# Bringing seven parts of x through ScalarE's DMA queue in a hybrid encoder layer

## The chip, the cores and the metric

The kernel runs on one core of a Trainium2 chip. The core has a matrix engine, TensorE (PE in the profile, with PEld for its weight loads), a vector engine, VectorE (DVE), ScalarE (ACT), GpSimd (POOL) and SyncE (SP). Each engine works through its own instruction queue in order. Data moves between the large memory (DRAM) and the on-chip memory by DMA; an engine's queue issues a DMA with an instruction of its own, and 16 DMA engines carry it out. Here SyncE issues nearly all DMAs and ScalarE issues some stores.

The metric is the time of one execution on the device in microseconds, as the median of several runs. Lower is better.

## The reference, cut to what matters

The kernel computes one layer of a bidirectional encoder for a sequence of 2048 positions and 1024 channels, in float32, and a final norm:

```python
h = rmsnorm(x, norm_w)                                   # x: 2048 x 1024
proj = h @ w_in                                          # w_in: 1024 x 10240, ten splits of 1024
q, f_fwd, f_bwd, i, g_a, u, v, g_b, m_a, m_b = split(proj)
# branch A: gated linear recurrence, 8 heads of 128, chunks of 64, forward and backward
k, log_f = forget(f, lower_bound)                        # per direction
state_t  = diag(f_t) state_{t-1} + k_t v_t^T ;  o_t = state_t^T q_t      # v is i
y_a = rmsnorm(o_fwd + o_bwd, gnorm_w) * silu(g_a)
# branch B: spatial gating over chunks of 128 positions
y_b = gelu(u) * (w_s @ layernorm(gelu(v)) + b_s) * silu(g_b)
merged = sigmoid(m_a) * (y_a @ w_proj_a) + sigmoid(m_b) * (y_b @ w_proj_b)
out = rmsnorm(x + merged @ w_out, final_norm_w)
```

Most of the work is in the products with `w_in`. The change lies in how the operand of these products that comes from h is brought on chip.

## The kernel before, in words

**Products.** Each large product is done in float16 with a high and a low half of each operand (three matmuls for one: high by high, high by low, low by high). It is also cut in 2 x 2 blocks by a scheme with seven block products in place of eight (`PRODUCTS`). Each of the seven needs one *part* on the x side: the blocks A11, A12, A22, and the sums S1 to S4 of blocks. A part holds 128 partitions x 8 KB, 1 MB in all. The sequence is cut into two halves, p = 0 and p = 1, and each has its own seven parts. They are made once at the start and kept in DRAM (`x_d`; the page calls the tensors `x` and `x_sums`, and the on-chip tile `xT`).

**Slots.** There are eight slots on chip for parts: seven in use and one spare. A *group* (`seven`, L1108) is seven products, in the order 0, 1, 2, 3, 5, 4, 6, for one unit of 256 weight columns and one half p. One product is `mm12` (L1171 holds the matmul): 12 matmuls of 128 x 512. Product 6 of a group is held back and done after the first two products of the next group (the "tail").

**Phases.** The value stage (`values`) and the recurrence (`recurrence`) go through groups of the same p in *phases*: the recurrence has nine phases, of two, then seven times three, then four groups, and p changes from each to the next. In the last group of a phase, as soon as a product has read a part for the last time, its slot is free, and the next part of the *other* p is loaded into it. `after` (L584) does this: it is called after each product of each group; if the group is the last of its phase (`end`), it takes the slot of the part just read and calls `x_fetch` (L578) for the part after it in `PARTS`. The seventh slot becomes the spare one. A11 of the other p goes into the spare slot, asked for at the beginning of the group before the last (L555). `after` also asks for pieces of the next group's weights (L586), on SyncE's queue.

**The recurrence beside it.** Between products, `pump` runs steps of the recurrence itself for one head, direction and segment of 512 positions at a time: operands (scans on VectorE, activations on ScalarE), scores on PE (`sc`), masking, state updates on PE (`pu`, L918) and outputs on PE (`po`). For the state updates the keys are needed transposed: `key_parts` copies kt to float16 on ScalarE (L839), takes the rest on VectorE (L840), and issues a DMA transpose into `ks` on SyncE's queue (L842). SyncE's queue in this stage also carries the stores and loads of intermediate outputs and scores (`of`, `o_d`, `at`) and of values (`v`).

**Copies out of PSUM.** A product's result leaves the accumulation memory (PSUM, tiles `bank`) by ScalarE: as a plain copy for products 0, 1 and 2 (L1119, which notes itself as `self.reads["act"]`), or with a scale at L605 in product 6; products 3, 5 and 4 leave by VectorE (L1207).

**What sets the order.** The framework's planner arranges each engine's instructions by their place in the program (which `high_priority` can raise) and by its own estimate of when each becomes ready, and puts in the semaphore waits. The order on each engine is then fixed. A DMA that overwrites a slot waits, in the queue of the engine that issues it, until the matmuls that read the slot are done. `tc.issue_after(ins)` puts the block's instructions on the engine of `ins` behind it.

Of the kernel before, what the change touches and what calls it, by code (L numbers as in the profile page):

```python
# [53 lines left out]
A11, S1, A12, A22, S3, S2, S4 = B11, T1, B21, B22, T2, T3, T4 = range(7)  # L54
# [5 lines left out]
class Trunk:  # L60
# [89 lines left out]
    def plan(self):  # L150

        w = self.w_in
        self.todo, self.us_i = [(w, C_I + U * hp) for hp in range(4)], {}
        self.made, self.hooks, self.reads, self.fill = [], [], {}, []
        self.reads_first, self.ahead_of, self.wt, self.junk, self.few = True, 0, None, None, {}
# [357 lines left out]
    def recurrence(self):  # L513
        nc, tc = self.nc, self.tc
        with ExitStack() as es:
            E = es.enter_context
            R = dict(side="right", reuse_waits="tile")
            self.c1 = E(tc.tile_pool(name="g_const", bufs=1, **R))
            self.gv = E(tc.tile_pool(name="g_v", bufs=2, **R))
            self.gq = E(tc.tile_pool(name="g_q", bufs=1, **R))  # L520
            self.gof = E(tc.tile_pool(name="g_of", bufs=7, **R))
            self.gat = E(tc.tile_pool(name="g_at", bufs=5, **R))
            self.gt = E(tc.tile_pool(name="g_t", bufs=2, **R))
            self.gs = E(tc.tile_pool(name="g_s", bufs=11, **R))
            self.zs = E(tc.tile_pool(name="zsr", bufs=9, reuse_waits="tile"))
            self.pk = E(tc.tile_pool(name="p_k", bufs=1, space=PSUM, reuse_waits="tile"))
            self.pq = E(tc.tile_pool(name="p_r", bufs=1, space=PSUM, reuse_waits="tile"))
            self.reads_first, self.ahead_of = False, READS
            self.q_free, self.q = [f"q{n}" for n in range(12)], {}
            self.fill, self.late_norm = [], None  # L530
            self.queue, self.state, self.kept_at, self.v_of, self.v_raw = [], {}, {}, {}, {}
            self.pipe, self.turn, self.credit, self.held_once = [None] * 2, 0, 0.0, False
            self.patterns()

            groups = []
            for hp in range(4):
                a, b = hp % 2, 1 - hp % 2
                if hp == 0:
                    groups.append([("q", 0, 0, 0, None), ("f", 0, 0, 1, None)])
                groups.append([("q", hp, 1, a, ("b", hp)), ("f", hp, 1, b, ("q", hp + 1) if hp < 3 else ("mb", 0)),  # L540
                               ("b", hp, 1, a, None)])
                if hp < 3:
                    groups.append([("q", hp + 1, 0, b, None), ("b", hp, 0, a, ("f", hp + 1)),
                                   ("f", hp + 1, 0, a, None)])
            groups.append([("b", 3, 0, 1, ("mb", 1)), ("mb", 0, 0, 0, ("mb", 2)), ("mb", 1, 0, 1, ("u", 0)),
                           ("mb", 2, 0, 0, ("gb", 0))])
            tail = None
            for n, phase in enumerate(groups):
                p, last = n % 2, n == len(groups) - 1
                for m, (kind, hp, _, slot, after) in enumerate(phase):  # L550
                    end = m == len(phase) - 1 and not last
                    g = self.r_group(kind, hp, p, slot)
                    done = partial(self.after, slot, after, p, end)
                    if m == len(phase) - 2 and not last:
                        self.x_fetch(1 - p, A11, self.spare)  # L555
                    first = list(self.ORDER[:2])
                    for i in self.ORDER[:2]:
                        next(g)
                        done(i)
                        self.pump()  # L560
                    if tail:
                        next(tail[0])
                        tail[1](6)
                        self.pump()
                    for i in self.ORDER[2:6]:
                        next(g)
                        done(i)
                        self.pump()
                    tail = g, done
            next(tail[0])  # L570
            tail[1](6)
            while self.queue or any(self.pipe):
                self.step_on(True)
            self.norms()
            self.X = [{c: self.slot_part(self.slot[p, c]) for c in self.PARTS} if p == 0 else {} for p in range(2)]
        self.reads_first, self.ahead_of, self.pq = True, 0, None

    def x_fetch(self, p, part, slot):  # L578
        self.nc.sync.dma_start(out=slot, in_=self.x_d[p][part])
        self.slot[p, part] = slot  # L580

    def after(self, slot, key, p, end, n):

        if key and n in self.LOADS:  # L584
            at = slice(*self.LOADS[n])
            self.nc.sync.dma_start(out=self.ws[slot][:, :, at], in_=self.pre[key].d[:, :, at])  # L586
        if end:
            i = self.ORDER.index(n)
            free = self.slot.pop((p, self.PARTS[i]))
            if i < 6:  # L590
                self.x_fetch(1 - p, self.PARTS[i + 1], free)
            else:
                self.spare = free

# [1713 lines left out]
```

## Time and profile before

| | |
|---|---|
| median of 3 runs | 2207.83 us (2206.01 to 2208.66) |
| profiled execution, its own time | 2207.17 us |
| its span, first to last instruction | 2205.4 us |
| mean granted clock of TensorE | 0.996 |
| TensorE / VectorE / ScalarE / GpSimd busy | 98% / 76% / 61% / 15% of the span |
| stores of the value stage's results (L1324) | issued from 216.5 to 350.1 us |
| transposes of the recurrence (L842) | 64, issued from 385.8 to 1024.9 us |

"Busy" is the time in which an engine's instructions run, as a share of the span. Each row of a group of instructions gives its line in the kernel, engine, operation, what it writes and reads, the count, busy time, the mean length of one in ns, and the idle time just before them with what ended it. A row of waits gives who waited, for whom, the total, how often, and the longest. In rows of the timeline the start and the length stand ahead. Engine names with a q (SPq, ACTq) are instructions of that engine's queue which occupy its sequencer alone, such as the issue of a DMA; "to landing" is the time from a DMA's issue until its data has arrived.

### The profile page before, as it was taken

The page shows a single profiled execution, that of the slowest core. Times are in us where ns is not written, and L with a number is a line of the kernel's source. Part 1 is how long each engine was busy: PE and PEld are TensorE (multiplying, and loading weights), DVE is VectorE, ACT ScalarE, POOL GpSimd, SP SyncE. Part 2 cuts the span into 40 slices and gives each one's busy share as a digit, 9 for nine tenths or more (in the row PEclk, how much of TensorE's full clock was granted, in tenths as well). Part 3 has the DMA queues.
Part 4 walks back from the last instruction along what each step waited for, and adds up shares of the span by engine and source line. Part 5 has one row for each costly group of instructions (what it writes and reads, how often), then busy time and mean ns, then how long its engine had stood idle before and what let it go on. Part 6 is the DMA issues. An engine that isn't in the chain of part 4 may idle for free.

```text
span 2205.4 us, 35017 instructions
## 1 busy us (share of the span) xinstructions
PE 2161.6 (98%) x12654; PEld 1216.1 (55%) x12654; DVE 1665.7 (76%) x3063; ACT 1347.2 (61%) x2740; POOL 338.0 (15%) x526
## 2 busy tenths in 40 slices
PE   8999999999999999999999999999999999999998
PEld 7887444666666666666454554444445444444444
DVE  6878965878999889988677684698864745687764
ACT  6577876767778778777465554676664622344442
POOL 2036643002303103213000000000000000000011
PEclk9999999999999999999999999999999999999999
DMA  8898996768768758867732224788756665877643
GB/s 324 335 354 313 360 376 249 192 177 256 217 161 255 221 154 237 251 168 216 251 112 94 82 86 148 286 291 315 285 178 206 239 234 185 280 262 281 247 157 105
DMA packets 269064, 503.91 MB, mean 228 GB/s; under 512 B 92496, under 2 KB 154192, under 8 KB 245200
## 3 DMA queue, kind: packets, MB, share of 16 engines
q1 hardware_dynamic: 245696, 459.36, 62.7%
q10 hardware_dynamic: 23184, 42.22, 5.1%
q8 instruction: 101, 1.65, 0.3%
q14 instruction: 83, 0.68, 0.1%
HBM read 317.74 MB, written 166.99 MB: 220 GB/s over the span
## 4 chain that ended last, share of the span: by engine, by line
PE 44%; issue 3%; DMA 2%; DVE 1%; ACT 0%; POOL 0%; SPq 0%; POOLq 0%; DVEq 0%; ACTq 0%
PE bank L1171 43%; PE px L1501 1%; DMA mg<-zs 1%; DVE seven L1071 1%; DMA raw<-mg 0%; PE px L1805 0%; DMA seven<-kept 0%; DVE zs L1207 0%; DMA zs<-mb 0%; ACT seven L1070 0%; DVE tmp L973 0%; ACT tmp L1021 0%; POOL wsb L1026 0%; DVE zs L1973 0%; DVE zs L1961 0%
## 5 line engine op out<-in xcount | busy, mean ns | idle before, releaser
L1171 PEld LDWEIGHTS <-seven 128*128 128x128 f16 x7404 | 722.8, 100 | 767.0 <-issue 10.3
L1171 PE MATMUL bank<-xT,seven 128*128 128x512 f16 x4116 | 972.1, 380 | 4.8 <-ACT zs L605 2.5
L1171 PE MATMUL bank<-seven 128*128 128x512 f16 (+1 forms) x2028 | 436.1, 378 | 1.0 <-DVE zs L2027 0.7
L1171 PE MATMUL bank<-xs,seven 128*128 128x512 f16 x1260 | 282.2, 379 | 0.0
L1207 DVE SCALAR_TENSOR_TENSOR zs<-bank,us,zs 128x512 f32<-128x512 f32 x192 | 142.7, 745 | 91.2 <-PE bank L1171 64.8
L1119 ACT ACTIVATE zs<-bank,us 128x512 f32<-128x512 f32 x192 | 130.2, 680 | 106.6 <-PE bank L1171 101.3
L1174 PEld LDWEIGHTS sc<-ff,kt 128*128 128x128 f32 x684 | 130.0, 190 | 47.8
L1215 ACT ACTIVATE zs<-zs 128x512 f32<-128x512 f32 x144 | 90.0, 627 | 102.8 <-DVE zs L1207 90.8
L1071 DVE SCALAR_TENSOR_TENSOR seven<-raw,ws,seven 128x1024 f16<-128x1024 f32 x80 | 111.1, 1419 | 50.8 <-ACT seven L1070 49.9
L1171 PE MATMUL bank<-seven,xT 128*128 128x512 f16 x672 | 146.5, 379 | 1.2 <-DVE zs L1207 1.2
L220 PE MATMUL pin<-wsplit,xT 128*128 128x256 f16 x512 | 140.2, 274 | 2.2 <-DVE xT L302 2.2
L219 PE MATMUL pin<-wsplit,xT 128*128 128x256 f16 x512 | 140.2, 274 | 0.9 <-DVE wsplit L208 0.9
L218 PE MATMUL pin<-wsplit,xT 128*128 128x256 f16 x512 | 140.4, 274 | 0.0
L1119 ACT ACTIVATE zs<-bank,su 128x512 f32<-128x512 f32 x72 | 49.0, 682 | 142.8 <-PE bank L1171 132.3
L850 ACT ACTIVATE q<-ff,e 128x64 f32<-128x64 f32 x512 | 131.6, 337 | 1.6 <-issue 0.4
L1174 PE MATMUL sc<-ff,kt 128*128 128x64 f32 (+1 forms) x684 | 119.2, 256 | 0.0
L1171 PEld LDWEIGHTS <-xT 128*128 128x128 f16 x672 | 64.6, 98 | 77.2 <-issue 1.5
L1207 DVE SCALAR_TENSOR_TENSOR zs<-bank,su,zs 128x512 f32<-128x512 f32 x72 | 53.8, 748 | 52.1 <-PE bank L1171 41.7
L1070 ACT ACTIVATE seven<-raw,ws 128x1024 f16<-128x1024 f32 x80 | 88.3, 1138 | 6.3 <-DVE ws L147 2.8
L1071 DVE SCALAR_TENSOR_TENSOR seven<-tmp,ws,seven 128x768 f16<-128x768 f32 x80 | 82.1, 1056 | 10.8 <-ACT seven L1070 10.4
L926 DVE SCALAR_TENSOR_TENSOR st<-st,e,pu 128x128 f32<-128x128 f32 x224 | 75.9, 339 | 6.0 <-PE pu L918 4.9
L1040 POOL TENSOR_TENSOR tmp<-raw 128x512 f32<-128x512 f32 x40 | 59.6, 1490 | 108.3 <-DVE seven L1071 40.1
(272 smaller groups left out, 3192.9 us busy)
## 6 DMA issues: line engine op xcount, KB each, us to landing
xT<-x_sums SPq DMA_DIRECT2D x41, 1024.0 KB, 7.1
raw<-in_w_in_dram SPq DMA_DIRECT2D x38, 1024.0 KB, 8.2
xT<-x SPq DMA_DIRECT2D x30, 1024.0 KB, 7.2
seven<-kept SPq DMA_DIRECT2D x15, 1792.0 KB, 9.1
kept<-seven SPq DMA_DIRECT2D x16, 1024.0 KB, 5.1
kept<-seven SPq DMA_DIRECT2D x16, 768.0 KB, 6.1
v<-v SPq DMA_DIRECT2D x20, 512.0 KB, 5.6
x<-xT SPq DMA_DIRECT2D x8, 1024.0 KB, 8.4
```

The lines of the kernel that those rows point to most:

```text
L218: nc.tensor.matmul(ps, lh(k), rh(k), start=start and k == 0, stop=False, skip_group_check=len(ks) < KT)
L219: nc.tensor.matmul(ps, lh(k), rl(k), start=False, stop=False, skip_group_check=len(ks) < KT)
L220: nc.tensor.matmul(ps, ll(k), rh(k), start=False, stop=k == KT - 1, skip_group_check=len(ks) < KT)
L850: self.nc.scalar.activation(out=q0[:, at], in_=ff[:, at], func=AF.Copy, scale=e8[:, n, b:b + 1])
L926: nc.vector.scalar_tensor_tensor(out=sn, in0=st, scalar=e8[:, n, last:last + 1], in1=pu[:, n, :], op0=ALU.mult, op1=ALU.add)
L1070: nc.scalar.activation(out=out[0], in_=src, func=AF.Copy, scale=s)
L1071: nc.vector.scalar_tensor_tensor(out=out[1], in0=src, scalar=s, in1=out[0], op0=ALU.mult, op1=ALU.subtract)
L1119: self.reads["act"] = self.nc.scalar.activation(out=t, in_=ps, func=AF.Copy, scale=su)
L1171: nc.tensor.matmul(ps, lhs(x, k), rhs(y, k), start=start and not (k or n), stop=k == 3 and n == 2, skip_group_check=True)
L1174: self.fill.pop(0)()
L1207: self.reads["dve"] = self.nc.vector.scalar_tensor_tensor(out=more, in0=ps, scalar=su, in1=more, op0=ALU.mult, op1=ALU.add)
L1215: self.nc.scalar.activation(out=out, in_=more, func=func)
```

## The change

`x_fetch` gets an argument by which it issues the load from ScalarE's queue. `after` and the phase loop no longer call it at once; they note the wanted load in `next_x`. A new function `x_next`, called at the beginning of each `after`, issues the noted load from ScalarE's queue, behind the newest plain copy out of PSUM. The loads of whole parts in the value stage's last group for p = 1 and in all phase changes of the recurrence go this way. The other callers of `x_fetch` (the loads at the start, A11 ahead of the recurrence, and those after the recurrence) stay on SyncE's queue.

```diff
     def plan(self):
+        self.next_x = None
...
                     if m == len(phase) - 2 and not last:
-                        self.x_fetch(1 - p, A11, self.spare)
+                        self.next_x = 1 - p, A11, self.spare
...
-    def x_fetch(self, p, part, slot):
-        self.nc.sync.dma_start(out=slot, in_=self.x_d[p][part])
+    def x_fetch(self, p, part, slot, beside=False):
+        (self.nc.scalar if beside else self.nc.sync).dma_start(out=slot, in_=self.x_d[p][part])
         self.slot[p, part] = slot
 
+    def x_next(self):
+
+        if self.next_x:
+            with self.tc.issue_after(self.reads["act"].ins):
+                self.x_fetch(*self.next_x, True)
+            self.next_x = None
+
     def after(self, slot, key, p, end, n):
 
+        self.x_next()
         if key and n in self.LOADS:
...
             free = self.slot.pop((p, self.PARTS[i]))
             if i < 6:
-                self.x_fetch(1 - p, self.PARTS[i + 1], free)
+                self.next_x = 1 - p, self.PARTS[i + 1], free
             else:
                 self.spare = free
```

## The prediction

> **What bounds the kernel now.** I read the page first: how busy each engine is, and what each hardware DMA queue carried (q1 is SyncE's, q10 ScalarE's).
>
> ```profile
> PE 2161.6 (98%) x12654; PEld 1216.1 (55%) x12654; DVE 1665.7 (76%) x3063; ACT 1347.2 (61%) x2740; POOL 338.0 (15%) x526
> q1 hardware_dynamic: 245696, 459.36, 62.7%
> q10 hardware_dynamic: 23184, 42.22, 5.1%
> ```
>
> TensorE (PE) is busy 98% of 2205.4 us. A change that adds and removes no matmul can only change PE's idle time and its clock, and may also add idle time. The second view is therefore PE's waits, from 250 us, ahead of the first load that moves, to 1045 us, where the recurrence is over.
>
> ```profile
> PE pu L918 <- DMA ks<-kt: 4.4, 2, 3.8
> PE bank L1171 <- ACT zs L605: 2.5, 3, 0.9
> PE po L946 <- DVE rfe L809: 1.3, 1, 1.3
> PE bank L1171 <- DVE zs L1207: 1.2, 1, 1.2
> PE po L942 <- ACT at L904: 0.6, 1, 0.6
> PE px L1078 <- ACT wsb L1028: 0.5, 2, 0.3
> PE po L942 <- DVE at L905: 0.5, 1, 0.5
> ```
>
> Columns: total us, times, longest. All together 11.0 us, and none of it on a part of x: no load that is moved is late today. The largest is ks, the transposed keys, which SyncE's queue brings by DMA transpose. It came late twice, once by 3.75 us. The third view is PE and its clock around that stall.
>
> ```profile
> 758.43 1.05 PE L946 MATMUL po<-st,q 128*128 128x128 f32 x8
> 763.24 1.46 PE L918 MATMUL pu<-v,ks 128*128 128x128 f16 x12 [3.75 <-DMA ks<-kt]
> 764.49 4.87 PE L1171 MATMUL bank<-xT,seven 128*128 128x512 f16 x13
> 772.47 2.97 PE L1171 MATMUL bank<-xT,seven 128*128 128x512 f16 x13
> 776.16 0.83 PE L918 MATMUL pu<-v,ks 128*128 128x128 f16 x12
> 759.00:764.00 5.00, 1.25 (x13) 1.06 (x12) 2.14 (x7) 3.12 (x11) 0.00 (x0) 0.75 1.18 241
> 764.00:769.00 5.00, 5.00 (x20) 2.17 (x19) 3.51 (x8) 2.09 (x5) 0.00 (x0) 0.57 0.97 399
> ```
>
> In the last two rows the columns after the length are the busy times of PE, weight load, DVE, ACT and POOL, then PE's granted clock, the DMA engines' share and GB/s. After the stall the clock falls to 0.57, and the same groups cost more: 12 matmuls 1.46 instead of 0.83 us, 13 matmuls 4.87 instead of 2.97 us. So this one late transpose costs 3.75 + 0.63 + 1.90 = 6.3 us. The other long stall nearby did not lower the clock:
>
> ```profile
> PE px L1501 <- ACT vs L1490: 3.1, 1, 3.1
> 1067.00:1072.00 5.00, 5.00 (x32) 2.53 (x31) 4.91 (x11) 2.87 (x5) 0.00 (x0) 1.00 0.38 111
> ```
>
> After 3.1 us the clock was 1.00. I take it that a stall clearly shorter than 3.1 us loses no clock.
>
> Why was ks late? The fourth view is the order on SyncE's queue, with VectorE's last step ahead of the transpose, and the landing times of transposes: over all 64, then that of this one (min/median/max).
>
> ```profile
> 753.79 1.30 SPq L579 DMA_DIRECT2D xT<-x  x1
> 756.34 0.33 SPq L766 DMA_DIRECT2D of<-of  x1
> 756.72 1.56 SPq L842 DMA_TRANSPOSE ks<-kt  x1
> 758.38 1.35 SPq L579 DMA_DIRECT2D xT<-x_sums  x1
> 756.31 0.68 DVE L840 TENSOR_TENSOR kt<-kt,kt 128x512 f16<-128x512 f32 x1
> L842 SPq DMA_TRANSPOSE ks<-kt x64: 1232/1275/6285, 385.8 to 1024.9; - x64
> DMA to landing us min/median/max: 3.0/3.9/10.0
> DMA to landing us min/median/max: 6.5/6.5/6.5
> ```
>
> The transpose was issued as soon as VectorE had its input (756.31 + 0.68 against 756.72), so SyncE did not issue it late. It landed in 6.5 us where the fastest takes 3.0, behind a part of x issued 2.9 us earlier.
>
> **The change, part by part.** The loads that move are those at L579 between 250 and 940 us: one set of six in the value stage, and seven in each of eight phase changes of the recurrence.
>
> ```profile
> L579 SPq DMA_DIRECT2D xT<-x_sums x36: 319/436/1737, 255.3 to 922.9; - x36
> L579 SPq DMA_DIRECT2D xT<-x x26: 319/442/1302, 265.6 to 928.3; - x26
> SPq L579 <- PE bank L1171: 35.5, 23, 4.8
> SPq L579 <- PE po L946: 5.0, 6, 2.4
> L1171 PE MATMUL bank<-xT,seven 128*128 128x512 f16 x2331 | 573.4, 380 | 2.5 <-ACT zs L605 2.5
> ```
>
> *Removed from SyncE:* 36 + 26 = 62 issues, about 62 x 0.44 = 27 us of issue, and 35.5 + 5.0 us of waiting for PE to be done with a slot. Other loads, stores and transposes stood behind these. The PE waits above name no other SyncE transfer than ks, so this is worth nothing by itself.
>
> *One product later.* The last row is PE's group in the recurrence (347 to 1060 us): 2331 / 12 = 194 products in 713 us, 3.7 us each. A slot that comes free is read again seven products on, 26 us later; less one product, 22 us remain. Against that stand the landing times of these loads, in the fullest phase change (740 to 785 us) and then in the value stage (255 to 276 us):
>
> ```profile
> DMA to landing us min/median/max: 5.9/7.7/10.7
> DMA to landing us min/median/max: 13.4/16.9/18.8
> ```
>
> All are under 22 us, so this costs nothing; the products between are the cover. Were that cover gone, PE would wait for x itself, which it never does today.
>
> *The transpose's landing.* With x on another queue, a transpose no longer has the megabytes of x ahead of it in its own queue, but it shares the DMA engines with them (share 1.18 in the row of 759 us). No row shows a transpose beside x on ScalarE's queue. The bounds are 3.0 us (free) and 6.5 us (as now). I take 3.9, the median over all 64, in whose company x is sometimes there and sometimes not. PE was free at 758.43 + 1.05 = 759.48; 756.72 + 3.9 = 760.62, so 1.1 us of stall would be left. That removes 2.6 us and, since 1.1 is far below 3.1, the 2.5 us of clock: 5.1 us. The bounds give 0 and 6.0 us. The second stall on ks (0.67 us) goes likewise: 0.7 us. Together 5.8 us.
>
> The Trainium skill ("DMA: Bandwidth & Descriptors", section "Issuing engines are not separate DMA queues") speaks against this: DMAs of all issuing engines run on the same 16 DMA engines, and another issuer saves only the time of issuing. By that the landing stays at 6.5 us and the 5.8 us are nothing; it is the second rival below. The same page ("Queues, rings and completion order") says that a DMA engine takes turns between the queues for which it has work, packet by packet, which would let a transpose past a long x load. No run so far shows which of the two counts here.
>
> *Added to ScalarE:* 62 issues, each with a semaphore instruction. The nearest rows are ScalarE's own DMA issues in the recurrence, and what one did to the instruction behind it:
>
> ```profile
> L614 ACTq DMA_DIRECT2D gb<-zs x12: 326/326/373, 971.8 to 1034.8; - x12
> 971.78 0.37 ACTq L614 DMA_DIRECT2D gb<-zs  x1
> 972.21 1.06 ACT L850 ACTIVATE q<-ff,e 128x64 f32<-128x64 f32 x4 [0.21 <-issue]
> 740.00:760.00 20.00, 19.49 (x133) 13.39 (x131) 17.97 (x50) 15.98 (x49) 3.60 (x10) 1.00 0.89 296
> ```
>
> 62 x 0.326 = 20.2 us in which ScalarE's sequencer does nothing else. In the busiest phase change (740 to 760 us) ScalarE idles 20 - 15.98 = 4.0 us; seven issues need 2.3 us, so on average they fit. Behind an issue stand the copy of kt (L839), which VectorE and then the transpose wait for, and the evictions (L1119, L605), which free PE's banks. PE already waits three times for L605, so there an issue adds its whole length: 3 x 0.33 = 1.0 us. Bounds: 0 (always in idle time) to 20.2 us (always on the path). I take 1.0, since PE shows ScalarE's lateness at these three places only.
>
> *The wait that comes with a load.* A load is queued behind the newest plain copy out of PSUM (`reads["act"]`). That copy covers PE's reading of the slot for five loads of seven, since it is the copy of the same or a later product. For S4 and S3 it does not: products 3 to 5 end on VectorE, and the newest copy is that of product 2. So ScalarE can stand still until PE is through with product 3 or 5. As it is asked one product later, I take 0; the upper bound is in the third rival.
>
> **Sum.** -5.1 - 0.7 + 1.0 = -4.8 us. The profiled execution took 2207.17 us (span 2205.4 and 1.8 around it), 0.7 below the median of the runs, 2207.83. So 2202.4 for such an execution, 2203.0 for the median.
>
> **Rivals.** *All long waits go.* Both ks stalls vanish to their bounds (6.0 + 0.7) and the three waits on L605 move away by luck (2.5): -9 us, 2199. For it: few stalls are left to remove. Against it: ScalarE gets more work, not less.
>
> *Nothing on the path.* The DMA engines are full at a phase change (1.18), the same megabytes land beside the transpose, and ks stays late; with +1.0 for ScalarE this is 2209. For it: that DMA share. Against it: the transposes' times follow what stands ahead of them, 3.0 when nothing does. A variant is that the planner issues the loads at other times and the stall only moves to another phase change: the same time.
>
> *ScalarE becomes the gate (slower).* The place is S4 and S3, two waits in each phase change. SyncE's 23 waits at L579 on a bank's product average 35.5 / 23 = 1.54 us. If ScalarE meets the same, a phase change costs it 2.3 us of issues and 3.1 us of waits, 5.4 against 4.0 us of idle time: 1.4 us too much, through kt and the evictions to PE. Eight phase changes give 11 us: 2219. It decides from (4.0 - 2.3) / 2 = 0.85 us a wait. For it: ScalarE's queue is in order, and VectorE has only 2 us of idle in those 20. Against it: ScalarE is itself paced by PE's products, while SyncE runs ahead of them.
>
> *The loads don't move as described:* each still has its slot's wait, and the planner may put it well behind its product; then nothing changes but chance: 2208.
>
> **How the numbers follow.** A measurement here can tell about 0.2%, 4.4 us, from no change: 2203.4 and 2212.2 are the borders. Chances: forecast 0.46 (own range 2199 to 2206, 0.36 of it below 2203.4), all waits go 0.06, nothing on the path 0.26 (0.03 of it beyond 2212.2), ScalarE the gate 0.20, not as described 0.02. Faster 0.36 + 0.06 = 0.42, the same 0.10 + 0.23 + 0.02 = 0.35, slower 0.03 + 0.20 = 0.23. The range goes from 2197 (the bound of 6.0 + 0.7 + 2.5 with no cost, and the runs' spread of some 1.5 us) to 2219 (the slower rival).
>
> **What would show it.** Right: 62 loads of x among ScalarE's DMA issues at about 0.33 us; ks landing below about 4.5 us where x is in flight; no wait of PE on ks over 1.5 us; clock 1.00 throughout the recurrence. Wrong: ks as late as now; waits on ScalarE (L605, at) or VectorE growing by more than 2 us in sum; ScalarE idle at the new loads for PE's products; a new drop of the clock after a stall over 3 us.

## The result, and the profile after

The changed kernel takes 2339.2 us (2325.9 to 2350.5, four runs) against 2206.9 us (2203.4 to 2208.7) for the kernel before. The ratio is 1.060, with a 95% interval of 1.058 to 1.062. So it is 132 us slower, where the forecast was 3 to 5 us faster.

The page of the kernel after begins with its span and its busy engines, and gives the two hardware queues.

```profile
span 2348.7 us, 34979 instructions
PE 2199.0 (94%) x12654; PEld 1215.0 (52%) x12654; DVE 1674.3 (71%) x3063; ACT 1342.0 (57%) x2740; POOL 345.2 (15%) x526
q1 hardware_dynamic: 236768, 394.34, 51.6%
q10 hardware_dynamic: 32112, 107.23, 13.2%
```

The loads moved as the diff says: 65 MB (the second column; 459.36 - 394.34) went from queue q1 to q10. Of the 143.3 us of longer span (2348.7 - 2205.4), 37.4 us is longer busy time of TensorE (2199.0 - 2161.6, same number of matmuls) and 105.9 us is new idle time. The stages show where. First the kernel after, then the kernel before; each row holds the value stage, then the recurrence, then the rest (columns as in the prediction).

```profile
250.00:360.00 110.00, 100.85 (x473) 44.96 (x472) 85.28 (x128) 76.35 (x118) 54.46 (x49) 0.98 0.84 326
360.00:1185.00 825.00, 716.98 (x4625) 442.87 (x4624) 609.08 (x1393) 505.01 (x1398) 141.55 (x259) 0.95 0.65 177
1185.00:2348.70 1163.70, 1146.34 (x5706) 540.58 (x5704) 782.84 (x1251) 590.21 (x974) 54.93 (x138) 1.00 0.59 206
```

```profile
250.00:347.00 97.00, 95.16 (x456) 43.03 (x452) 74.12 (x119) 71.15 (x111) 46.99 (x41) 1.00 0.90 356
347.00:1045.00 698.00, 688.21 (x4642) 447.55 (x4640) 609.85 (x1404) 515.85 (x1415) 141.54 (x269) 1.00 0.73 211
1045.00:2205.40 1160.40, 1142.91 (x5696) 538.84 (x5695) 781.87 (x1247) 588.07 (x964) 52.25 (x135) 1.00 0.59 206
```

The recurrence took 825 us in place of 698, which is 127 of the 143 us. VectorE and ScalarE do nearly the same work there as before (609 and 505 us, before 610 and 516); TensorE idles 108 us of it, where it idled 10, and its clock averages 0.95. TensorE's waits from 250 to 1185 us say for what (total us, times, longest):

```profile
PE pu L927 <- DMA ks<-kt: 81.6, 28, 17.2
PE sc L1183 <- DVE ff L836: 16.5, 22, 2.3
PE bank L1180 <- DVE zs L1216: 6.6, 2, 6.0
PE bank L1180 <- ACT zs L1222: 4.2, 2, 2.2
PE bank L1180 <- DMA xT<-x_sums: 2.3, 2, 1.4
```

The parts of x themselves cost 2.3 us. It is the transposed keys, ks, that are late: 28 times and 81.6 us, where it was twice and 4.4 us. The worst case, in the timeline of the kernel after with the landing times of this transpose and of the three x loads beside it (min/median/max):

```profile
628.20 1.05 PE L955 MATMUL po<-st,q 128*128 128x128 f32 x8
646.47 1.46 PE L927 MATMUL pu<-v,ks 128*128 128x128 f16 x12 [17.22 <-DMA ks<-kt]
620.03 0.33 ACTq L580 DMA_DIRECT2D xT<-x  x1
621.71 3.02 SPq L851 DMA_TRANSPOSE ks<-kt  x1
622.10 0.34 ACTq L580 DMA_DIRECT2D xT<-x_sums  x1
625.80 0.33 ACTq L580 DMA_DIRECT2D xT<-x_sums  x1
635.00:640.00 5.00, 0.00 (x0) 0.00 (x0) 0.00 (x0) 0.00 (x0) 0.00 (x0) 0.50 1.25 138
DMA to landing us min/median/max: 24.7/24.7/24.7
DMA to landing us min/median/max: 11.4/21.5/21.7
```

The transpose was issued between loads of x from ScalarE's queue. All of them became slow: 24.7 us for the transpose, 11.4 to 21.7 us for the loads. In the middle of it the DMA engines read as full (1.25) while they move 138 GB/s; the row of 759 us in the prediction, with x and a transpose on one queue, had 241 GB/s at 1.18.

But few of the 28 waits look like that, and the fastest and the median transpose are as quick as before:

```profile
L851 SPq DMA_TRANSPOSE ks<-kt x64: 1233/1268/3794, 405.0 to 1166.9; - x64
DMA to landing us min/median/max: 3.0/3.7/24.7
```

There are 64 sets of keys, so each step of the preparation can be paired, in order, with its transpose and with the state update (`pu`) that reads it. One ordinary set of keys in the kernel after: ScalarE's copy, VectorE's remainder, the transpose, the state update.

```profile
695.54 0.63 ACT L848 ACTIVATE kt<-kt 128x512 f16<-128x512 f32 x1
698.40 0.69 DVE L849 TENSOR_TENSOR kt<-kt,kt 128x512 f16<-128x512 f32 x1
699.11 1.25 SPq L851 DMA_TRANSPOSE ks<-kt  x1
702.22 0.84 PE L927 MATMUL pu<-v,ks 128*128 128x128 f16 x12
```

And one in the kernel before:

```profile
642.13 0.63 ACT L839 ACTIVATE kt<-kt 128x512 f16<-128x512 f32 x1 [0.37 <-DVE kt L818]
643.87 0.68 DVE L840 TENSOR_TENSOR kt<-kt,kt 128x512 f16<-128x512 f32 x1
644.62 1.25 SPq L842 DMA_TRANSPOSE ks<-kt  x1
659.81 0.83 PE L918 MATMUL pu<-v,ks 128*128 128x128 f16 x12
```

Before, the keys are through VectorE 15 us ahead of their use (659.81 - 644.55) and have lain there 11.8 us. After, 3.1 us ahead, just the transpose's own time. Over all 64 sets the median time from landing to use, called the *slack* below, fell from 9.9 us to less than 0.1. That points to a change of the order in which each engine does its work, and the diff's own lines hold no such thing. The experiments therefore had to part the queue from the order.

### The profile page after: what moved, and what is told of

Its sections match the earlier page's. It is cut to its first block, busy times and chain, and to the rows that moved or that the text cites. A ratio compares the mean times of both kernels' runs of the same rounds, so it can differ in the third digit from the quotient of the medians.

```text
span 2348.7 us, 34979 instructions
## 1 busy us (share of the span) xinstructions
PE 2199.0 (94%) x12654; PEld 1215.0 (52%) x12654; DVE 1674.3 (71%) x3063; ACT 1342.0 (57%) x2740; POOL 345.2 (15%) x526
## 3 DMA queue, kind: packets, MB, share of 16 engines
q1 hardware_dynamic: 236768, 394.34, 51.6%
## 5 line engine op out<-in xcount | busy, mean ns | idle before, releaser
L1183 PEld LDWEIGHTS sc<-ff,kt 128*128 128x128 f32 x684 | 110.7, 192 | 57.3 <-DVE ff L836 23.5
L927 PE MATMUL pu<-v,ks 128*128 128x128 f16 x720 | 55.0, 229 | 81.9 <-DMA ks<-kt 81.6
L1183 PE MATMUL sc<-ff,kt 128*128 128x64 f32 (+1 forms) x684 | 108.1, 268 | 16.6 <-DVE ff L836 16.5
L927 PEld LDWEIGHTS <-ks 128*128 128x128 f16 x720 | 46.0, 102 | 96.8 <-DMA ks<-kt 95.0
```

Source lines behind the costliest of these rows:

```text
L927: nc.tensor.matmul(pu[:, n, :], ks[:, 4 * x + n, :], v[:, y, n, hs], start=m == 0, stop=m == 2)
L1183: self.fill.pop(0)()
```

## The experiments

All ratios are to the kernel before, with 95% intervals. "Order" means the sequence of instructions on an engine, the loads of x left out. The kernel before has 33016 instructions on TensorE's list; the kernel after has another one at 1469 of these places.

### Which part of the edit

**delay**: the loads stay on SyncE's queue and are issued one product later.

```diff
-            with self.tc.issue_after(self.reads["act"].ins):
-                self.x_fetch(*self.next_x, True)
+            self.x_fetch(*self.next_x)
```

> The loads of x stay on SyncE's queue and are only asked for one product later. Theory 1 (the queue): the loss of 132 us comes from 1 MB loads that run on ScalarE's queue beside the transposes on SyncE's; then this is within 0.3% of the kernel before, about 2207 us, with ks waits of PE under 8 us in sum. Theory 2 (the order): the planner's new order of all engines makes the loss; it puts only 58 of PE's 33016 places and 60 of VectorE's 4648 differently here, so again about 2207. Theory 3 (lateness): parts of x that come one product later do the harm; then over 2280.

**dummy**: the kernel before, with a small store of a constant (64 KB) from ScalarE's queue, behind the newest plain copy, wherever the change has a load.

```diff
+            with self.tc.issue_after(self.reads["act"].ins):
+                self.nc.scalar.dma_start(out=self.dump[self.next_x - 1], in_=self.ones)
```

> The kernel before, and beside each of the 62 loads a 64 KB store of a constant from ScalarE's queue, one product later, behind the newest copy. PE's order is that of before; VectorE's differs in 72 places. Theory 1 (queue): no large load on ScalarE's queue, about 2210 us. Theory 2 (order): about 2210. Theory 4 (ScalarE's time): 62 issues of 0.33 us in ScalarE's queue cost most of the loss through kt and the evictions: over 2250.

**pool**: delay, but from GpSimd's queue.

```diff
-        self.nc.sync.dma_start(out=slot, in_=self.x_d[p][part])
+        (self.nc.gpsimd if beside else self.nc.sync).dma_start(out=slot, in_=self.x_d[p][part])
```

> The loads of x one product later on GpSimd's queue. PE's order differs from before in 94 places (after: 1469). Theory 1 (queue): whole 1 MB parts run beside the transposes on a queue of their own, so ks lands late as in after: 2300 us or more, with ks landings over 12 us. Theory 2 (order): the order is nearly that of before, so 2200 to 2225 us.

**split2**: the kernel after, with half of each part on each queue.

```diff
+            self.nc.scalar.dma_start(out=slot[:, :2], in_=src[:, :2])
+            self.nc.sync.dma_start(out=slot[:, 2:], in_=src[:, 2:])
```

> Of each part of x, one half (512 KB) on ScalarE's queue and the other half on SyncE's, both one product later. PE's order differs in 102 places from before, VectorE's in 650. Theory 1 (queue): half the bytes run beside the transposes on the other queue, so a good part of the loss: 2240 to 2300 us, some ks landings over 10 us. Theory 2 (order): 2200 to 2230 us, ks landings as before (up to 10 us).

| kernel | median us | ratio | TensorE places changed |
|---|---|---|---|
| delay | 2201.3 | 0.998 (0.997 to 0.999) | 58 |
| dummy | 2213.4 | 1.003 (1.002 to 1.004) | 0 |
| pool | 2259.0 | 1.023 (1.021 to 1.025) | 94 |
| split2 | 2216.2 | 1.005 (1.003 to 1.006) | 102 |

The delay costs nothing and gains a little. The 62 issues on ScalarE, their waits and the little stores together cost 0.3%. Neither explains 6%. In dummy's trace part even of this small cost falls on the keys: TensorE's waits for ks, in the stretch where the kernel before has 4.4 us, are

```profile
PE pu L934 <- DMA ks<-kt: 8.4, 4, 3.9
```

and one transpose lands in 12.5 us. GpSimd's queue, with an order nearly that of before, costs 2.3%, so on both engines tried a second queue has a price. pool's 2259 us lies between the two theories, above what the order allowed (2225) and below what the queue alone was to cost (2300). TensorE's wait for ks, the issues of the 64 transposes (shortest, median and longest in ns) and their landing in pool:

```profile
PE pu L926 <- DMA ks<-kt: 41.1, 5, 11.5
L850 SPq DMA_TRANSPOSE ks<-kt x64: 1232/1274/16531, 392.4 to 1076.8; - x64
DMA to landing us min/median/max: 3.0/4.3/32.4
```

Few and long waits, and transposes of up to 32.4 us, as in the worst case of the kernel after. The issue of a transpose alone took up to 16.5 us, against at most 6.3 us before; what stands behind it on SyncE's queue starts only after it. In split2, with 512 KB a part on ScalarE's queue, the planner hardly changed TensorE's order (VectorE's at 650 of 4648 places), and most of the loss is not there: 2216 us, where the theory of the queue had 2240 or more, with transposes of up to 13.9 us.

### Is it the transposes that suffer beside x

**pool256**, **after256** and **before256**: pool, after and before with the transpose replaced by two plain copies of the same bytes in runs of 256. The keys reach the state update untransposed in these three.

```diff
-        nc.sync.dma_start_transpose(out=g["ks"], in_=kt16.rearrange("p a n c -> p (a n c)"))
+        for a in range(2):
+            nc.sync.dma_start(out=g["ks"][:, 4 * a:4 * a + 4], in_=kt16.rearrange("p a n c -> p (a n) c")[:, a::2])
```

> The kernel with x on GpSimd's queue (ratio 1.023 to before), with the transpose into ks replaced by two plain copies of 128 KB in runs of 256 bytes, so ks holds untransposed data and the output is not the reference's. PE, VectorE, ScalarE and GpSimd keep the same order as with the transposes. Theory 1a (a transpose and loads of another queue hold each other up): no landing of ks over 10 us, PE waits on ks under 10 us in sum, about 2205 to 2215 us. Theory 1b (any stream of small packets on SyncE's queue is held up by 8 KB packets of another queue): ks still lands in 15 to 30 us in some phase changes, 2240 us or more.

> Control: the kernel before with the same plain copies in place of the transposes (output not the reference's). Both theories: 2195 to 2207 us, since the copies are issued in less time and the one late transpose is gone.

> The changed kernel with the same plain copies (output not the reference's); its order is that of after but for 508 of PE's 33016 places. Theory 1a alone (transposes beside another queue are the whole loss): within 0.5% of the control, about 2210 us. Theory 2 beside it (the planner's new order costs by itself what the x-on-GpSimd kernel, with before's order, did not lose): 2250 to 2290 us, with many short waits of PE on ks and on VectorE's ff.

Measured: before256 1.000 (0.999 to 1.001), so the exchange by itself is free; pool256 1.005 (1.003 to 1.007); after256 1.052 (1.049 to 1.054). On GpSimd's queue the price falls from 2.3 to 0.5%: most of it is the transposes beside x. (The copies there still landed in up to 14.8 us, above the 10 expected.) In the kernel after it falls only from 6.0 to 5.2%, and after256 is slower still than the 2250 to 2290 us expected of the order. TensorE's waits in after256:

```profile
PE pu L928 <- DMA ks<-kt: 46.3, 23, 7.5
PE sc L1184 <- DVE ff L836: 19.2, 21, 2.7
```

Plain copies that land in 2.7 us at the median are late just the same. This part does not hang on the transpose; it is the order.

### Order and queue apart

**act_old** is the kernel after with the order of all five engines held to that of before until the end of the recurrence; only the loads of x stand free. **sp_new** is delay with the order of all five engines held to that of the kernel after. No run holds the order of the kernel before on that kernel itself, to see what the holding costs; pe_first below, held on TensorE alone, came to 1.007. The order is held by dependencies between neighbours on the same engine, which add no wait:

```diff
+            for a, b in zip(order[:-1], order[1:]):
+                self.tc.add_manual_dep(made[e][b], made[e][a].name, mybir.DependencyInfo(
+                    mybir.DependencyClass.NoSync, mybir.DependencyReason.DATA), reason="order")
```

> The changed kernel (x on ScalarE's queue, one product later), but the order of every other instruction, on all five engines up to the end of the recurrence, is held by edges to be exactly that of the kernel before. Theory 2 (the planner's new order makes most of the loss): 2215 to 2265 us; what is left over 2207 is ScalarE's issues and x beside the transposes. Theory 5 (x on ScalarE's queue costs as much in any order): 2320 us or more.

> x on SyncE's queue, one product later, with the order of every other instruction, on all five engines up to the end of the recurrence, held to be exactly that of the changed kernel. Theory 2 (order): slow without any load of x on ScalarE's queue, 2270 to 2320 us. Theory 5 (ScalarE's queue): about 2201 to 2215 us, as the kernel with the delay alone.

**act_old256** is act_old with the plain copies of 256-byte runs for the transpose (keys untransposed), held on all engines but SyncE.

> As the changed kernel in the order of before (held on PE, VectorE, ScalarE and GpSimd), with the transpose into ks replaced by two plain copies in runs of 256 bytes (output not the reference's). Theory 1a (transposes beside another queue): faster than the same with transposes by what x beside transposes costs, 10 to 45 us; no landing of ks over 12 us. If transposes don't matter on ScalarE's queue: the same time within 5 us.

| | x on SyncE's queue | x on ScalarE's queue |
|---|---|---|
| order of before | 0.998 (delay) | 1.026 (1.023 to 1.030, act_old) |
| order of after | 1.050 (1.048 to 1.052, sp_new) | 1.060 (1.058 to 1.062, after) |

The new order alone costs 5.2 points, without one byte on ScalarE's queue. The queue alone costs 2.8 points. Together they cost 6.2, less than the sum; that a set of keys late for both reasons is waited for once would explain it, and was not tested. TensorE's waits for ks, in act_old and in sp_new:

```profile
PE pu L952 <- DMA ks<-kt: 38.5, 3, 23.6
```

```profile
PE pu L951 <- DMA ks<-kt: 45.4, 21, 10.5
PE sc L1207 <- DVE ff L860: 19.4, 23, 2.6
```

The two kinds of loss look different: the queue gives three waits of up to 23.6 us, the order gives 44 waits of about 1.5 us. act_old256 came to 1.013 (1.011 to 1.015), and TensorE waits for ks for 0.5 us in all. So of the queue's 65 us over delay (2266.6 - 2201.3) the transposes beside x make 34 (2266.6 - 2232.6). That act_old256 leaves SyncE's order free is a second difference between the two. Of the other 31 us, dummy accounts for at most some 6, and its loss was itself on ks. The trace of act_old256 shows where some of the rest may lie, at the loads on ScalarE:

```profile
854.25 6.79 ACTq L604 DMA_DIRECT2D xT<-x_sums  x2
861.15 0.63 ACT L872 ACTIVATE kt<-kt 128x512 f16<-128x512 f32 x1 [8.17 <-DMA of<-of]
PE bank L1205 <- ACT zs L638: 8.4, 7, 3.5
```

ScalarE stood at the loads of two sums for 6.8 us, and the copy of the next keys came 8.2 us late behind them. The profile puts the end of this wait down to the landing of a transfer of SyncE's queue, not to TensorE's products; why a load of x should wait for that was not followed up. TensorE's waits for the copies at L638 are 8.4 us, where delay has 1.7 for the same copies. No run isolates any of this, so what the rest is stays open.

### More delay

**delay2** and **delay3**: delay with two and three products between.

```diff
-                self.next_x = 1 - p, self.PARTS[i + 1], free
+                self.next_x.append([2, 1 - p, self.PARTS[i + 1], free])
```

> All loads on SyncE's queue, asked for two products later instead of one. If the gain of the one-product delay (ratio 0.998) comes from x standing less often right ahead of a transpose, two products may give as much or a little more, 2195 to 2205 us; if parts of x begin to come late, PE waits on xT appear and it is over 2207 us.

> All loads on SyncE's queue, three products later. One product later gave a ratio of 0.9976, two 0.9972. If the gain is the spacing from the transposes, 2195 to 2205 us; if parts come late now, PE waits on xT and over 2207 us.

Measured 0.997 (0.996 to 0.998) and 0.998 (0.997 to 0.999). The three delays are alike and all beat the kernel before by 0.2 to 0.3%. The cover is real: even three products later, where some 15 of the 26 us are left (four products of 3.7 us), TensorE waits for no load of x.

### Which engine's order

Four kernels more, each with one engine's order held and the planner free to arrange the others around it, except **sp_order**, where the other four are held to delay's. **pe_first** and **act_first** are delay with TensorE's or ScalarE's order of the kernel after. In act_first the planner moves VectorE's order too, towards that of the kernel after. **act_held** is the kernel after with ScalarE's order of before.

```diff
-ORDER = {'SP': ..., 'Pool': ..., 'DVE': ..., 'PE': ..., 'Activation': ...}
+ORDER = {'Activation': ...}
```

> x on SyncE's queue one product later; TensorE, VectorE, ScalarE and GpSimd keep the order of the kernel delay, and only SyncE's instructions other than these loads are held to the order of after. Theory A (keys are prepared too late because VectorE and ScalarE do the preparing instructions later against TensorE's products): SyncE's order costs nothing by itself, 0.996 to 1.002; the median time from the landing of a transpose to the state update that reads it stays near delay's 9.9 us. Theory B (the place of the transposes among SyncE's stores and loads makes them late): most of the 5 points, 1.03 or more, with a median slack below 3 us.

> x on SyncE's queue one product later; only TensorE's order is held to that of after, and the planner orders the others around it (they come out near delay's order). Theory A: TensorE's order alone is not the cause; 1.00 to 1.015, median slack of the keys 6 us or more. Theory C (TensorE's order has the scores and state updates too early among the products): 1.03 or more, median slack below 3 us.

> x on SyncE's queue one product later; only ScalarE's order is held to that of after, and the planner orders the others around it (VectorE comes out near after's order, TensorE between the two). Theory A: nearly the whole price of after's order, 1.035 to 1.055, median slack of the keys below 3 us, TensorE waiting for ks by 25 us or more. Theories B and C: below 1.02.

> after, x on ScalarE's queue, with ScalarE's order alone held to that of before; the planner orders the others and re-sorts TensorE and VectorE. If ScalarE's order is what makes the keys late: near the kernel with all orders held, 1.026 (1.02 to 1.035), median slack 7 us or more. If VectorE's or TensorE's new order is enough: 1.045 to 1.06, median slack below 4 us.

Measured, with three figures worked out over the 64 sets of keys of each trace: products that TensorE does between VectorE's last step and the state update (matmuls into `bank` between the two, divided by 12), mean time from that step to the transpose's issue, and the median slack.

| kernel | ratio | products | to issue, us | slack, us |
|---|---|---|---|---|
| before | 1 | 4.2 | 1.8 | 9.9 |
| act_old | 1.026 | 4.1 | 2.1 | 9.1 |
| pe_first | 1.007 (1.005 to 1.009) | 4.2 | 1.8 | 9.3 |
| act_held | 1.029 (1.026 to 1.032) | 2.9 | 0.3 | 6.0 |
| act_first | 1.034 (1.031 to 1.037) | 1.7 | 0.2 | 0.6 |
| sp_order | 1.045 (1.043 to 1.047) | 4.6 | 10.8 | 2.0 |
| sp_new | 1.050 | 1.7 | 0.3 | 0.1 |
| after | 1.060 | 1.7 | 0.2 | 0.0 |

TensorE's order is not the main cause: alone it costs 0.9 points over delay. Theory A failed on sp_order and theory B on act_first (which came out a shade under A's 1.035). SyncE's order alone is enough to use up the slack, and so is ScalarE's order together with what the planner makes of VectorE's around it; the two were not parted, and what makes up the 1.6 points between act_first and sp_new was not followed up. In act_first the keys come through VectorE 2.5 products later than before. In sp_order they come through VectorE as early as ever, but the transposes stand 10.8 us in SyncE's queue, behind loads of weights whose slot TensorE has not freed yet. SyncE's waits there, from 250 to 1100 us, and one case from 640 to 660 us:

```profile
SPq L619 <- PE bank L1204: 225.3, 47, 19.3
```

```profile
640.57 0.69 DVE L873 TENSOR_TENSOR kt<-kt,kt 128x512 f16<-128x512 f32 x1
652.16 0.59 SPq L619 DMA_DIRECT2D seven<-pre_f  x1
654.21 1.59 SPq L875 DMA_TRANSPOSE ks<-kt  x1
658.11 0.68 PE L951 MATMUL pu<-v,ks 128*128 128x128 f16 x9 [2.50 <-DMA ks<-kt]
```

The keys were ready at 641.3; SyncE waited 19.3 us for a bank's product, loaded the weights at 652.16, and only then came to the transpose.

The kernel after has the other form. ScalarE's waits for products of TensorE at its plain copies, in the kernel after and in the kernel before:

```profile
ACT zs L1128 <- PE bank L1180: 127.7, 44, 26.7
```

```profile
ACT zs L1119 <- PE bank L1171: 16.4, 12, 3.1
```

ScalarE comes to a copy out of PSUM before the product is done, stands there, and what follows on its queue stands behind it, in places the preparation of the next keys:

```profile
683.79 0.69 ACT L1128 ACTIVATE zs<-bank,us 128x512 f32<-128x512 f32 x1 [1.02 <-PE bank L1180]
684.38 0.62 ACT L848 ACTIVATE kt<-kt 128x512 f16<-128x512 f32 x1
```

sp_new has the same row with 129.8 us in 47 waits and act_first with 102.9 us in 41, without x on ScalarE's queue. The longest of 26.7 us is no cause, though: it spans TensorE's own stall of 17.2 us. Given back ScalarE's old order alone (act_held), the kernel falls to 1.029, although TensorE's matmuls, compared by tile and shape, still come in another order at 1073 of 12654 places of the trace (1082 in the kernel after). So giving it back takes away about half of the 6.0%. That 1.029 is near the price of the queue with all orders held (1.026) is in part chance: TensorE waits for ks 12 times and 29.3 us in act_held, 3 times and 38.5 us in act_old. Its slack of 6.0 us is a little under the 7 expected.

What made the planner choose the new order was not run on the chip, and only the orders themselves speak on it: delay (58 places on TensorE), dummy (none) and split2 (102) leave TensorE's nearly alone, and the whole part on ScalarE's queue does not. So neither the later issue nor the issues and waits on ScalarE bring it about; that the planner counts the bytes of a load as time on the queue that issues it would fit, and is only argued.

## Why the prediction was wrong

**The bound.** Right as far as it went: TensorE sets the time, no x load is late before the change, and none matters after it (2.3 us).

**The sum had no term for the order.** This is the larger failure. The prediction treats the change as 62 moved loads among otherwise fixed instructions, and where it does name the planner, in the variant of the rival *Nothing on the path*, it says that loads issued at other times give "the same time", and in *The loads don't move as described* that nothing changes but chance. In fact the planner re-sorted all engines, and that alone cost 5.2 points, about 113 us (2314.3 - 2201.3). The row on which the forecast rested also held the warning: ks was what TensorE waited for most, and the prediction read it as two stalls to be removed, not as the margin that 62 other sets of keys lived on. It never worked out that margin, 9.9 us at the median.

**The transpose's landing.** Wrong in sign. Put at 3.9 us between bounds of 3.0 and 6.5; with x on another queue transposes landed in up to 24.7 us, and with the order held this cost some 34 us instead of gaining 5.8. The upper bound was taken from one landing on a shared queue, although the whole set already had 10.0 us. What the stalls on ks were worth was not far off: in delay2 and delay3 TensorE's waits name ks no more and both gain 5.9 us, which agrees with the 5.8 of the sum, though no run isolates it. They went by later loads on the same queue, not by another queue.

**The clock after short stalls.** The prediction took it that a stall clearly shorter than 3.1 us loses no clock. That fails. In the kernel after a wait of 2.27 us was enough:

```profile
982.99 2.63 PE L1183 MATMUL sc<-ff,kt 128*128 128x128 f32 x12 [2.27 <-DVE ff L836]
983.00:988.00 5.00, 5.00 (x34) 4.75 (x35) 3.48 (x8) 3.05 (x10) 0.09 (x1) 0.66 0.49 99
```

The same 12 matmuls take 1.55 us at 697.93 us. The kernel before had such a case too, outside the views that the prediction took: a wait of 2.90 us ends at 136.94 us, and from 137 to 141 us the granted clock is 0.59. So a stall shorter than 3.1 us can cost clock, and the price of the many short waits in the new order had no term in the sum either.

**The Trainium skill on queues.** "DMA: Bandwidth & Descriptors", section "Issuing engines are not separate DMA queues", says that another issuer saves only the time of issuing. It spoke rightly against the gain. But it names no price, and the runs show one: GpSimd's queue cost 2.3% and ScalarE's 2.6% in an order hardly or not changed. The turn-taking in its section "Queues, rings and completion order", which the prediction thought might let a transpose past a long load, did not do so here: transposes of up to 24.7 us in the kernel after.

**Removed from SyncE.** Not tested by itself. SyncE's queue did lose the 62 issues, but its waits for a bank's product ahead of weight loads grew from 53.1 us (23 waits) to 144.4 us (37). The transposes were issued 0.2 us after their input in place of 1.8, but that is the new order: with the order of before held it is 2.1 us (act_old), so no relief of theirs shows.

**One product later.** Right: delay, delay2 and delay3 lose nothing, and gain 0.2 to 0.3%.

**Added to ScalarE.** The length of an issue was right: the rows of the moved loads in the kernel after are

```profile
L580 ACTq DMA_DIRECT2D xT<-x_sums x36: 326/326/1134, 259.9 to 1058.0; - x36
L580 ACTq DMA_DIRECT2D xT<-x x26: 326/326/341, 269.0 to 1065.9; - x26
```

Dummy, with as many issues and waits, cost 0.29%, some 6 us, where 1.0 was taken; that is within the bounds of 0 to 20.2 us, but 4.0 us of it are more waits for ks (8.4 against 4.4), and its waits on the copies of L605 are 0.4 us, where the kernel before has 2.5: the path that the prediction took does not show.

**The rivals.** *ScalarE becomes the gate* had the right engine, but not the mechanism of most of the loss: ScalarE holds up the keys by its copies out of PSUM in the new order, and sp_new has that without any load on ScalarE's queue. ScalarE standing at loads of sums is there too (6.8 us for two loads in act_old256, above), though that longest case ended with a transfer and not with a product, and what it cost was not isolated. It priced this at 11 us, against 132. *All long waits go* and *nothing on the path* both assumed that ks could not get worse.

**What would show it.** The marks were well chosen: 62 loads at 0.33 us came true; ks below 4.5 us, no wait over 1.5 us and a clock of 1.00 all failed (24.7 us, 17.2 us, 0.50 in the row of 635 us).

## What to carry to other kernels

Where a planner orders the engines, an edit that moves megabytes between queues is an edit of every engine's order: compare the order of all engines before pricing the moved instructions, and hold it if the edit is meant to be local. For each operand that is made just ahead of its use, work out the slack from landing to use over all its instances, not only at the stalls that show; an operand with 9.9 us of slack behind an in-order queue is a bottleneck one reordering away. Keep DMA transposes and large loads on one queue, or at least measure a transpose beside a load on another before counting on its landing time.

## What the runs showed of the hardware that was not expected

A DMA transpose and plain 1 MB loads slow each other when they come from different queues: transposes of 24.7 us (ScalarE, after), 26.3 us (ScalarE, act_old) and 32.4 us (GpSimd, pool) against at most 10.2 us when both are on SyncE's queue (before, the three delays and pe_first), with loads of x of up to 28.3 us in act_old against 10.5 in delay (from 340 us on). Part of the transpose's time is its issue, up to 14.5 us in act_old and 16.5 in pool, in which SyncE's queue does nothing else. Plain copies of the same bytes in runs of 256 did not suffer like that: at most 14.8 us in pool256 and 11.4 in act_old256, with 3.3 us of TensorE's waits in the first and 0.5 in the second, and the loads of x beside them landed in at most 11.2 and 10.6 us. Why the two kinds of transfer disturb each other across queues was not found out; the traces show DMA engines that read as full (1.25 at 635 us in the kernel after) while they move 138 GB/s.

A long stall also costs after it ends. In the stall of 17.2 us the granted clock went down to 0.50, and the 12 matmuls behind it took 1.46 us in place of 0.84. Over the recurrence the clock averaged 0.95, and TensorE's busy time there, 29 us longer than before (716.98 - 688.21), goes with it. Nor is a long stall needed: the wait of 2.27 us above was followed by a clock of 0.66, where one of 3.1 us in the kernel before was followed by 1.00.
